# Every fourth weight slab's low part on GpSimd, in a transformer block pair of split-precision matmuls

## The chip, the cores and the metric

One core of a Trainium2 chip. The time is device microseconds of one execution of the whole program; several runs of the kernel are timed, and one more execution is taken with the hardware profiler. TensorE (PE) multiplies, VectorE (DVE), ScalarE (ACT) and GpSimd (POOL) do elementwise work, and DMA queues are issued from SyncE (SP), ScalarE and GpSimd. PEld in the profile is TensorE's loading of weights.

## The reference

Two transformer blocks on 256 tokens of width 2048, all in float32. What matters here is that nearly all of the work is products of a 256 x K activation with a large weight matrix:

```
# block 1
proj = rms_norm(x) @ w_in                     # 2048 x 7168
mixed = concat(diff_attention, hgrn2) @ w_out # 2048 x 2048
x = x + rms_norm(mixed)
x = x + rms_norm(cross_attention(x, mem))     # w_cq, w_ckv, w_co
x = x + rms_norm((silu(h @ w_gate) * (h @ w_up)) @ w_ffn_out)   # hidden 5632
# block 2
z = rms_norm(x) @ w_in_2                      # 2048 x 11280
y = gates_a * (pool_mixer @ w_branch_a) + gates_b * (gated_linear_attention @ w_branch_b)
x = x + rms_norm(y @ w_out_2)
x = x + rms_norm((silu(h @ w_ffn_gate) * (h @ w_ffn_up)) @ w_ffn_down)
```

Each weight element is used once for each of the 256 tokens, so all weights (some 0.5 GB) pass through SBUF once.

## The kernel before

**The matmuls.** A float32 product is made of three products of reduced type (float32r): with each operand split into a high part, which is the value rounded, and a low part, which is the rest, it is high x high + high x low + low x high. Activations are split when they are transposed (`split_T`, lines 307 to 324: ScalarE makes the high part, VectorE the low part). Weights are split as they arrive.

**Slabs.** A slab is 256 rows (two chunks of 128) by 512 columns of a weight matrix, 512 KB. `wsub` (lines 367 to 377) fetches one: SyncE issues the DMA into a `raw` buffer (line 371), ScalarE casts it into the high part `wh` (line 375), and VectorE subtracts to make the low part `wl` (line 376). There are four `raw` buffers and eight each of `wh` and `wl` (lines 33 and 34), taken in rotation. A raw buffer can be refilled when its cast and its subtraction are done; a `wh` or `wl` buffer when TensorE has used it.

**Groups.** `group` (lines 385 to 395) computes 512 columns of the output for both halves of the tokens (two tiles of 128): it asks for all slabs of the group, eight of them where K is 2048 (six or four elsewhere), and then multiplies. `mm_both` (lines 397 to 410) goes through the slabs once and does both token tiles for each chunk: 2 chunks x 3 products x 2 tiles = 12 matmuls a slab. With `apart` it is `mm` (lines 413 to 426): all slabs for tile 0, then all for tile 1, which is used at the boundaries between sublayers, where the second tile's input is not there yet.

**Order.** The kernel is written in one stream, and a scheduler puts each engine's instructions in the order of priorities, as far as their inputs are expected to be ready. `ahead` (lines 379 to 383) gives the slabs of a group a priority 50 instructions earlier than the place where they stand, so that they are prepared during the group before; at a boundary (`self.bound`) it gives them none. Each engine's queue, and each DMA queue, is in order when it runs. Beside the matmuls run small jobs that advance by a `tick` after every chunk: the decay attention (`decay_attn`, lines 506 to 596, called the lanes below), the softmax attention (lines 678 to 732), transposes, norms and the gating of the FFN (line 908). The lanes use VectorE at lines 535, 541, 543 and 550 and TensorE at line 516.

**Boundaries.** Between sublayers the outputs of a group are squared and summed, normalised with `rsqrt_mean` (lines 283 to 296) and added to x on VectorE (`add_normed`, lines 484 to 491, line 490), transposed on TensorE (line 304) and split (lines 322 and 323), before the next weight product can begin.

**GpSimd.** It sets a few buffers at the start, makes the identity, and issues DMAs: the setup vectors (line 195), the bias table (lines 263 and 273), the rows of mem (line 785), the broadcast gains (line 279) and the spilled x (line 948). It does no elementwise work on the weights.

Of the kernel before, what the change touches and what calls it, by code (L numbers as in the profile page):

```python
# [10 lines left out]
F32 = mybir.dt.float32  # L11
# [3 lines left out]
ALU = mybir.AluOpType  # L15
# [66 lines left out]
class Builder:  # L82
    def __init__(self, ctx, tc, A, out):
        self.tc, self.nc, self.A, self.out = tc, tc.nc, A, out
        e = ctx.enter_context
        self.cp = e(tc.tile_pool(name="const", bufs=1))
        self.ap = e(tc.tile_pool(name="acts", bufs=ACT_UNITS))
        self.rawp = e(tc.tile_pool(name="raw", bufs=RAW_BUFS))
        self.spp = e(tc.tile_pool(name="split", bufs=SPLIT_BUFS))
        self.smp = e(tc.tile_pool(name="small", bufs=16))  # L90
        self.psm = e(tc.tile_pool(name="psm", bufs=4, space=bass.MemoryType.PSUM))
        self.pss = e(tc.tile_pool(name="pss", bufs=4, space=bass.MemoryType.PSUM))
        self.n = 0
        self.junk = self.cp.tile([P, CW], F32, name="junk")
        self.jobs, self.lane, self.bound = [], [], False

# [270 lines left out]
    def wsub(self, W, k0, c0, ncol=CW):  # L367

        nc = self.nc
        raw = self.rawp.tile([P, 2, CW], F32, name=self.nm("raw"), tag="raw")  # L370
        nc.sync.dma_start(raw[:, :, :ncol],
                          W[k0 * P:(k0 + 2) * P, c0:c0 + ncol].rearrange("(k p) n -> p k n", p=P))
        hi = self.spp.tile([P, 2, CW], F32R, name=self.nm("wh"), tag="wh")
        lo = self.spp.tile([P, 2, CW], F32R, name=self.nm("wl"), tag="wl")
        nc.scalar.copy(hi[:, :, :ncol], raw[:, :, :ncol])  # L375
        nc.vector.tensor_tensor(lo[:, :, :ncol], raw[:, :, :ncol], hi[:, :, :ncol].bitcast(F32), ALU.subtract)  # L376
        return hi, lo

    def ahead(self):
# [782 lines left out]
```

## Time and profile before

| what | value |
|---|---|
| median of 3 runs | 2867.55 us (2867.44 to 2868.36) |
| the profiled execution, its own time | 2868.51 us |
| span of the profile, first to last instruction | 2866.7 us |
| TensorE matmul busy | 2836.1 us (99%) |
| VectorE busy | 1619.9 us (57%) |
| ScalarE busy | 1412.8 us (49%) |
| GpSimd busy | 44.7 us (2%) |
| read from HBM | 522.86 MB, 184 GB/s over the span |
| mean granted TensorE clock | 0.998 |

How to read it: busy time is the time in which an engine had an instruction under way. TensorE is covered to 99%, which by itself does not say that it runs at its peak, since the ends of matmuls are modelled; but where it is covered without a gap, another engine's saving cannot shorten the run. In the rows below, a timeline row gives the start, the duration, the engine and line, the operation, out<-in by the program's names and the number of instructions merged; in square brackets stands how long the engine had been idle before and what ended that.

### The profile page before, as it was taken

What the parts mean: (1) busy time and instruction counts of PE and PEld (TensorE: products, weight loads), DVE (VectorE), ACT (ScalarE), POOL (GpSimd) and SP (SyncE); (2) the same over time, 40 slices, a digit from 0 to 9 for tenths busy, and PEclk for the clock granted to TensorE, in tenths of its full rate; (3) what the DMA queues carried; (4) which work ended last, traced back from release to release, by engine and by line L of the source; (5) the groups of instructions that cost most, each with busy time, mean ns of one, the idle gap of its engine ahead of it and who ended that gap; (6) DMA issues with size and microseconds to landing.
All of it is one profiled execution on the core that took longest, in us unless ns stands there. A gap on an engine that the chain in (4) does not pass through costs nothing.

```text
span 2866.7 us, 35013 instructions
## 1 busy us (share of the span) xinstructions
PE 2836.1 (99%) x13196; PEld 2351.4 (82%) x13196; DVE 1619.9 (57%) x2147; ACT 1412.8 (49%) x2100; POOL 44.7 (2%) x89
## 2 busy tenths in 40 slices
PE   8999999999999999999999999999999999999998
PEld 6788888778888888888888898888888888888887
DVE  6666586665444455456665566555565444555455
ACT  6554575664444443445655475444464444443443
POOL 1000000000000000000000000000000000000000
PEclk9999999999999999999999999999999999999999
DMA  7555546546656666665655557666747666666663
GB/s 236 164 176 165 179 157 205 172 129 207 192 190 196 187 190 192 194 202 186 200 154 166 159 151 215 196 194 192 231 138 233 187 192 194 186 190 194 195 201 121
DMA packets 274922, 530.94 MB, mean 185 GB/s; under 512 B 17513, under 2 KB 29413, under 8 KB 274752
## 3 DMA queue, kind: packets, MB, share of 16 engines
q1 hardware_dynamic: 269040, 512.70, 58.6%
q0 software_dynamic: 5136, 14.95, 1.7%
q8 instruction: 103, 1.69, 0.2%
q10 hardware_dynamic: 576, 1.05, 0.1%
q14 instruction: 67, 0.55, 0.1%
HBM read 522.86 MB, written 5.77 MB: 184 GB/s over the span
## 4 chain that ended last, share of the span: by engine, by line
PE 94%; ACT 2%; DMA 1%; DVE 1%; issue 1%; SPq 0%; DVEq 0%; ACTq 0%
PE mm L407 83%; PE tp L304 2%; PE lps L516 2%; PE mm L422 2%; PE mm L423 2%; PE mm L424 2%; ACT junk L299 1%; ACT hi L322 1%; DVE wl L376 1%; DMA raw<-w_ffn_in 1%; ACT wh L375 0%; PE po L581 0%; PE sc L686 0%; DMA raw<-w_in 0%; DMA x<-x 0%
## 5 line engine op out<-in xcount | busy, mean ns | idle before, releaser
L376 DVE TENSOR_TENSOR wl<-raw,wh 128x1024 fp32r<-128x1024 f32 (+1 forms) x968 | 1176.0, 1216 | 1076.8 <-ACT wh L375 1074.6
L375 ACT CAST wh<-raw 128x1024 fp32r<-128x1024 f32 (+1 forms) x968 | 1012.1, 1047 | 1184.3 <-PE mm L407 1092.7
L407 PE MATMUL mm<-wh,hi 128*128 128x512 f32 (+1 forms) x3504 | 1091.5, 392 | 0.0
L407 PE MATMUL mm<-wl,hi 128*128 128x512 f32 (+1 forms) x3504 | 1080.0, 389 | 0.0
L407 PE MATMUL mm<-wh,lo 128*128 128x512 f32 (+1 forms) x3504 | 1077.6, 388 | 0.0
L407 PEld LDWEIGHTS mm<-wh,lo 128*128 128x128 f32 x3504 | 657.1, 188 | 133.8 <-issue 0.2
L407 PEld LDWEIGHTS mm<-wl,hi 128*128 128x128 f32 x3504 | 656.5, 188 | 132.0 <-issue 0.5
L407 PEld LDWEIGHTS mm<-wh,hi 128*128 128x128 f32 x3504 | 648.6, 188 | 129.9 <-issue 5.8
L422 PE MATMUL mm<-wh,hi 128*128 128x512 f32 (+1 forms) x304 | 121.6, 400 | 1.4 <-ACT hi L322 0.9
L423 PE MATMUL mm<-wl,hi 128*128 128x512 f32 (+1 forms) x304 | 120.1, 395 | 0.3 <-DVE wl L376 0.2
L424 PE MATMUL mm<-wh,lo 128*128 128x512 f32 (+1 forms) x304 | 119.8, 394 | 0.0
L322 ACT ACTIVATE hi<-tp,vec 128x128 fp32r<-128x128 f32 x224 | 71.7, 381 | 12.4 <-DVE lo L323 8.2
L323 DVE SCALAR_TENSOR_TENSOR lo<-tp,vec,hi 128x128 fp32r<-128x128 f32 x224 | 68.3, 345 | 15.9 <-ACT hi L322 15.1
L422 PEld LDWEIGHTS mm<-wh,hi 128*128 128x128 f32 x304 | 57.8, 190 | 16.5 <-ACT hi L322 6.5
L424 PEld LDWEIGHTS mm<-wh,lo 128*128 128x128 f32 x304 | 57.6, 189 | 13.0 <-DVE lo L323 2.2
L423 PEld LDWEIGHTS mm<-wl,hi 128*128 128x128 f32 x304 | 57.9, 191 | 11.4 <-DVE wl L376 1.6
L516 PEld LDWEIGHTS lps<-qd,kd 128*128 128x128 f32 x448 | 58.3, 191 | 4.2 <-issue 0.3
L516 PE MATMUL lps<-qd,kd 128*128 128x64 f32 x448 | 56.2, 268 | 0.0
L333 ACT ACTIVATE tok<-mm,r 128x512 f32<-128x512 f32 x44 | 30.1, 690 | 33.6 <-PE mm L407 33.6
L903 ACT ACTIVATE sg<-mm,r 128x512 f32<-128x512 f32 x44 | 30.4, 690 | 28.8 <-PE mm L407 28.8
L312 ACT CAST hi<-tp 128x512 fp32r<-128x512 f32 x54 | 29.6, 589 | 21.5 <-PE tp L304 21.4
L535 DVE TENSOR_TENSOR e<-b 128x512 f32<-128x512 f32 x56 | 38.3, 683 | 0.0
(241 smaller groups left out, 1181.7 us busy)
## 6 DMA issues: line engine op xcount, KB each, us to landing
raw<-w_in SPq DMA_DIRECT2D x256, 512.0 KB, 3.7
raw<-w_ffn_in SPq DMA_DIRECT2D x176, 512.0 KB, 3.8
raw<-w_ffn_out SPq DMA_DIRECT2D x88, 512.0 KB, 3.7
raw<-w_ffn_gate SPq DMA_DIRECT2D x88, 512.0 KB, 3.7
raw<-w_ffn_up SPq DMA_DIRECT2D x88, 512.0 KB, 3.7
raw<-w_ffn_down SPq DMA_DIRECT2D x88, 512.0 KB, 3.8
raw<-w_out SPq DMA_DIRECT2D x64, 512.0 KB, 4.2
raw<-w_branch_b SPq DMA_DIRECT2D x32, 512.0 KB, 3.8
```

What stands on the lines that cost most here:

```text
L304: self.nc.tensor.transpose(ps[:, i, :], src[:, i * P:(i + 1) * P], self.ident)
L322: nc.scalar.activation(hi[:, i, :], ps[:, i, :], AF.Copy, scale=g)
L323: nc.vector.scalar_tensor_tensor(lo[:, i, :], ps[:, i, :], g, hi[:, i, :].bitcast(F32), ALU.mult, ALU.subtract)
L375: nc.scalar.copy(hi[:, :, :ncol], raw[:, :, :ncol])
L376: nc.vector.tensor_tensor(lo[:, :, :ncol], raw[:, :, :ncol], hi[:, :, :ncol].bitcast(F32), ALU.subtract)
L407: nc.tensor.matmul(ps[t][:, :ncol], hT[t][kk // 4][p][:, kk % 4, :], w[:, i, :ncol], start=kk == first and p == 0 and w is wh, stop=kk == ...
L422: nc.tensor.matmul(ps[:, :ncol], xh, wh[:, i, :ncol], start=kk == first, stop=False)
L423: nc.tensor.matmul(ps[:, :ncol], xh, wl[:, i, :ncol], start=False, stop=False)
L424: nc.tensor.matmul(ps[:, :ncol], xl, wh[:, i, :ncol], start=False, stop=kk == last)
L516: nc.tensor.matmul(ps[:, h, :], lhs[:, i, :], rhs[:, i, :], start=c == 0, stop=c == cph - 1)
L535: nc.vector.tensor_tensor(ev, bv, bv[:, :, hh - 1:hh].to_broadcast([P, 4 * nb, 2 * hh]), ALU.subtract)
L903: nc.scalar.activation(u, ps, AF.Silu, scale=rstd[t])
```

## The change

Low parts of weight slabs are counted in the order in which the program asks for them; every fourth is computed on GpSimd instead of VectorE, by the same instruction on the same operands. Nothing else is touched.

```diff
-        self.n = 0
+        self.n = self.nsub = 0
...
         nc.scalar.copy(hi[:, :, :ncol], raw[:, :, :ncol])
-        nc.vector.tensor_tensor(lo[:, :, :ncol], raw[:, :, :ncol], hi[:, :, :ncol].bitcast(F32), ALU.subtract)
+        self.nsub += 1
+        eng = nc.gpsimd if self.nsub % 4 == 0 else nc.vector
+        eng.tensor_tensor(lo[:, :, :ncol], raw[:, :, :ncol], hi[:, :, :ncol].bitcast(F32), ALU.subtract)
         return hi, lo
```

## Rows read from the trace of the kernel before

**Rows 1.** The head of the page: busy us, share of the span, instructions of an engine.
```profile
span 2866.7 us, 35013 instructions
PE 2836.1 (99%) x13196; PEld 2351.4 (82%) x13196; DVE 1619.9 (57%) x2147; ACT 1412.8 (49%) x2100; POOL 44.7 (2%) x89
```

**Rows 2.** The waits of PE: us in total, times, longest us.
```profile
PE tp L304 <- DVE hh L908: 1.8, 1, 1.8
...
PE tp L304 <- DVE mg L490: 0.9, 1, 0.9
...
PE mm L423 <- DVE wl L376: 0.2, 1, 0.2
```

**Rows 3.** The waits of all engines, the longest of them.
```profile
ACT wh L375 <- PE mm L407: 1092.7, 705, 2.8
```

**Rows 4.** The chain that ended last, in the first FFN: start us, us.
```profile
753.01 43.54 PE mm L407 x192
```

**Rows 5.** The page's costliest groups: busy, mean ns | idle before, releaser.
```profile
L376 DVE TENSOR_TENSOR wl<-raw,wh 128x1024 fp32r<-128x1024 f32 (+1 forms) x968 | 1176.0, 1216 | 1076.8 <-ACT wh L375 1074.6
```

**Rows 6.** The groups of POOL: its one instruction that reads SBUF.
```profile
masks.py:199 POOL TENSOR_SCALAR_AFFINE_SELECT ident<-ident 128x128 f32<-128x128 f32 x1 | 0.3, 283 | 0.0
```

**Rows 7.** The page's DMA issues: xcount, KB each, median us to landing.
```profile
raw<-w_ffn_gate SPq DMA_DIRECT2D x88, 512.0 KB, 3.7
```

**Rows 8.** The timeline of the start: ACT, PE and POOL.
```profile
16.52 1.05 ACT L375 CAST wh<-raw 128x1024 fp32r<-128x1024 f32 x1
...
25.15 1.11 PE L304 MATMUL tp<-ident,x 128*128 128x128 f32 x4 [3.09 <-DMA x<-x]
...
28.48 1.04 ACT L375 CAST wh<-raw 128x1024 fp32r<-128x1024 f32 x1 [0.25 <-DMA raw<-w_in]
...
25.03 0.51 POOL L195 DMA_DIRECT2D vec_rows<-cross_pre_g  x1 [20.12 <-DVE vec_rows L192]
...
32.65 0.54 POOL L233 DMA_DIRECT2D onehot<-c_onehot  x1
...
34.13 0.39 PE L423 MATMUL mm<-wl,hi 128*128 128x512 f32 x1
```

**Rows 9.** The timeline of the boundary into the first FFN: ACT, DVE and PE.
```profile
616.36 1.15 ACT L375 CAST wh<-raw 128x1024 fp32r<-128x1024 f32 x1
...
619.43 1.22 DVE L376 TENSOR_TENSOR wl<-raw,wh 128x1024 fp32r<-128x1024 f32 x1
...
620.82 0.15 DVE L487 TENSOR_REDUCE pssq<-acc 128x1 f32<-128x4 f32 x1
...
619.50 0.50 PE L423 MATMUL mm<-wl,hi 128*128 128x512 f32 x1 [0.22 <-DVE wl L376]
...
621.01 0.39 PE L423 MATMUL mm<-wl,hi 128*128 128x512 f32 x1
...
623.25 0.99 PE L304 MATMUL tp<-ident,mg 128*128 128x128 f32 x5 [0.91 <-DVE mg L490]
```

**Rows 10.** The timeline of DVE at the end of a group in the first FFN.
```profile
790.87 1.22 DVE L376 TENSOR_TENSOR wl<-raw,wh 128x1024 fp32r<-128x1024 f32 x1 [1.49 <-ACT wh L375]
793.59 1.23 DVE L376 TENSOR_TENSOR wl<-raw,wh 128x1024 fp32r<-128x1024 f32 x1 [1.50 <-ACT wh L375]
```

**Rows 11.** The groups of DVE: the lanes' instructions with two SBUF inputs.
```profile
L535 DVE TENSOR_TENSOR e<-b 128x512 f32<-128x512 f32 x56 | 38.3, 683 | 0.0
...
L543 DVE TENSOR_TENSOR qd<-fT,e 128x256 f32<-128x256 f32 x56 | 23.5, 419 | 0.0
```

**Rows 12.** The timeline of a lane's step: its product on DVE, and PE's load.
```profile
150.63 0.42 DVE L543 TENSOR_TENSOR qd<-fT,e 128x256 f32<-128x256 f32 x1
...
151.44 0.54 PEld L516 LDWEIGHTS lps<-qd,kd 128*128 128x128 f32 x3
```

## The prediction

> **What bounds the kernel now.** I read the head of the page first, then TensorE's own waits, then the stretches in which it waits. TensorE (PE) is busy for 2836.1 of 2866.7 us, VectorE (DVE) for 57% of the span, GpSimd (POOL) for 44.7 us [rows 1]. So the work that the change moves is on an engine that has room, and goes to one that is nearly empty; neither is the bound. The waits of TensorE say how much a faster VectorE could return at most: 1.8 us on a product of line 908, 0.9 us on the normalised rows of line 490, and 0.2 us, once in the whole run, on a low part [rows 2]. That is 2.9 us for the rows that name VectorE with a price worth having.
>
> Why the low parts are never late: ScalarE, which makes the high part, waited 705 times for TensorE's matmuls, 1092.7 us in all [rows 3]. It waits for one of the eight split buffers. A slab is 12 matmuls, and 192 matmuls (16 slabs) take 43.54 us [rows 4], so a slab is consumed in 2.72 us. A buffer that comes free is filled at once and read seven slabs later, 19.0 us. Less the cast (1.05 us) and the subtraction (1.22 us, the mean of all 968 is 1216 ns [rows 5]) some 16.8 us are left. Only where a group gets no head start (the start, and the four boundaries between sublayers) can a low part be needed as soon as it is made.
>
> **What the change does, and the price of one.** 968 low parts [rows 5], every fourth: 242 instructions leave VectorE, 242 x 1.216 = 294 us, and 242 come to GpSimd. No operand, buffer or DMA is added. The counter runs in program order and most groups have eight slabs, so it is the fourth and eighth of a group, and always the same of the four raw buffers. What one costs on GpSimd the trace does not show. GpSimd's only instruction that reads SBUF took 283 ns for 128 elements of one input [rows 6], so 1024 elements would be 8 x 283 = 2.3 us as a plain multiple, and 4.5 us if a second input doubles it. From below, nothing in the rows makes it faster than VectorE's 1.2 us. I take 2.3 us, the plain multiple, and keep 1.2 and 4.5 as ends. The Trainium skill (GPSIMD Engine Reference, Performance versus the Vector engine) gives 4497 ns for 2048 elements of this kind; half of that is an estimate of 2.25 us, and no run here shows it.
>
> **Steady groups: 0.** 2.3 instead of 1.2 us comes out of 16.8 us of cover; even 4.5 us does. GpSimd is then busy 242 x 2.3 = 557 us, a fifth of the span. If the cover were gone, each of the 242 would cost its 1.1 us, 266 us. The queue of loads (SP) must now wait for GpSimd before it refills every fourth raw buffer, and it is in order, so three later loads stand behind that one. A turn of the ring is 4 x 2.72 = 10.9 us, and needs 3.7 us of landing [rows 7], 1.05 us of cast and 2.3 us: 7.1 us, with 3.8 us to spare.
>
> **GpSimd's own queue: 0.** Its DMA issues can now stand behind a low part that waits for its high part. The broadcast rows are asked for a group (21.8 us) ahead of use. The eight loads of mem (line 785) are used two ticks later and are the exposed ones: 0 to 8 x 2.3 = 18 us if each is met. TensorE has no wait on them now, so I take 0.
>
> **Start: +0.7.** The fourth slab's high part ends at 16.52 + 1.05 = 17.57 us, GpSimd has nothing to do until 25.03, so its low part ends near 19.9 us (22.1 at the upper end); TensorE next stands still until 25.15 us for the second half of x [rows 8]. Hidden. The eighth: its high part ends at 28.48 + 1.04 = 29.52, but GpSimd is issuing setup DMAs until 32.65 + 0.54 = 33.19, and TensorE reads that low part at 34.13. In front of those issues it ends at 31.8 and costs 0; behind them at 35.5, +1.4 us (at 4.5 us a piece 37.7, +3.6). I take the middle of the two orders, +0.7, and keep 0 to +3.6.
>
> **Boundary into the first FFN: -0.9.** The last slab there (the 184th) has its high part at 616.36 + 1.15 = 617.51, but VectorE reaches it only at 619.43 and ends at 620.65, with TensorE reading at 621.01 [rows 9]. GpSimd would start at 617.5 and end at 619.8: earlier, though each one is slower. VectorE loses the 1.22 us that stand in front of the sum of line 487, from which the 0.91 us wait for line 490 follows; I take all 0.9 back. The bad end: the 183rd slab is what TensorE already waited 0.22 us for; if GpSimd's instruction holds VectorE up until 619.8, that subtraction ends at 621.1 where TensorE had it at 619.50, +1.6 us.
>
> **Attention lanes: +1.** There VectorE's queue is dense and its products go to TensorE soon. The move takes 1.2 us of every four slabs off VectorE, a gain that rows 2 have nothing to pay for. Bounds 0 to +27, from the second rival; I take +1, near zero, since the waits of TensorE contain no lane matmul.
>
> **Sum.** 0.7 - 0.9 + 1 = +0.8 us. The profiled execution took 2868.51 us (its span is 2866.7), so 2869.3 by its clock; it stands 0.96 above the median of 2867.55, so on the medians' scale the forecast is 2868.4 us.
>
> **Rivals.** (1) *VectorE's relief pays at the boundaries.* Every wait in rows 2 goes: 2867.55 - 2.9 = 2864.6. It needs no low part late anywhere. To be faster by more than 0.2% it would need 5.7 us, twice what these rows hold, so it would have to come from a better order of TensorE's instructions. Against it: the other 2836.1 us are TensorE's busy time, which the change does not touch.
>
> (2) *A wait takes the place of the work removed: GpSimd's low part blocks VectorE in the lanes.* Mechanism: both read SBUF, and while GpSimd holds the read, a VectorE instruction with two SBUF inputs stands still. In the FFN there is room: low parts stand 2.72 us apart (790.87, 793.59 [rows 10]), and what VectorE does in between at a group's end (lines 908 and 313) has one operand in PSUM. In the lanes lines 535 and 543 run 112 times with two SBUF inputs [rows 11]. GpSimd is busy 2.3 of every 10.9 us, 21%; 112 x 0.21 = 24 are met, for half of 2.3 us on average: 27 us of delay on VectorE. It decides where TensorE wants the product within that 1.15 us: one product ends at 151.05 and the weight load of line 516 starts at 151.44, 0.39 us later [rows 12], and then the rest is a stall. All of them: 2895. Half of them, the case I price: +13.5, 2881.9. A third: +9, 2877. For it: such thin margins. Against: VectorE's queue is also 1.2 us shorter per four slabs, which the same lane gets back. The Trainium skill (SBUF — State Buffer, Who interferes with whom) says that a VectorE instruction with two SBUF inputs contends with a GpSimd instruction that reads SBUF and that the later of the two blocks fully. By that rule this is the likelier way; no row of the kernel before can show it, since its GpSimd runs nothing of the kind beside VectorE.
>
> (3) *GpSimd becomes the bound.* From 10.9 - 3.7 - 1.05 = 6.1 us per low part the ring of raw buffers stalls TensorE; at 7 us it would be 242 x 0.9 = +218 us. It needs nearly three times my price.
>
> **Chances.** No change that can be measured (0.2%, 5.7 us, is about what a measurement of this kernel can tell): 0.74. Slower: 0.20, nearly all of it (2), with 0.02 for (3). Faster: 0.06. The likeliest case alone spans 2864.6 (rival 1) to 2867.55 + 3.6 + 1.6 + 1 = 2873.8. The range reaches up to 2878, past a third of the lanes' delay; above it lie (3) and half of (2), about 0.1, and below it the few cases of a better order.
>
> **What would show it.** Right: line 376 on GpSimd 242 times at 2 to 3 us; VectorE down by some 290 us; TensorE's busy time unchanged; the wait of ScalarE for TensorE still the longest. Rival 2: VectorE's lines 376, 535, 541 and 543 with longer means than now, and new waits of TensorE on lane products. Rival 3: TensorE waiting for wl on GpSimd in the FFN. I am wrong if TensorE's waits on VectorE and GpSimd together grow by more than 6 us, or if the span falls below 2861.

## The result: slower by 1.45%, and the profile after

| what | before | after |
|---|---|---|
| median of 3 runs | 2867.55 us | 2908.51 us (2908.04 to 2908.98) |
| ratio, 95% interval | | 1.0145, 1.0130 to 1.0159 |
| the profiled execution, its own time | 2868.51 us | 2908.04 us |
| span of the profile | 2866.7 us | 2906.2 us |
| mean granted TensorE clock | 0.998 | 0.995 |

The forecast was 2868.4 us with a range to 2878.0; the time came out 41 us above the kernel before and 30.5 us above the range. From line 378 on, line numbers after are two higher than before.

The head of the page after, to be read against [rows 1]:

```profile
span 2906.2 us, 35034 instructions
...
PE 2842.2 (98%) x13196; PEld 2356.3 (81%) x13196; DVE 1413.7 (49%) x1905; ACT 1413.1 (49%) x2100; POOL 624.7 (21%) x331
```

The work moved as the diff says, and GpSimd is far from full. But the span grew by 39.5 us, TensorE's busy time by only 6.1, and VectorE's fell by 206 us although 294 us of work had left it. The low parts themselves, in the page's costliest groups (busy, mean ns, then the idle time ahead of them):

```profile
L378 DVE TENSOR_TENSOR wl<-raw,wh 128x1024 fp32r<-128x1024 f32 (+1 forms) x726 | 888.2, 1225 | 1177.6 <-ACT wh L375 1176.1
...
L378 POOL TENSOR_TENSOR wl<-raw,wh 128x1024 fp32r<-128x1024 f32 (+1 forms) x242 | 581.3, 2402 | 2216.4 <-ACT wh L375 2216.4
```

One low part takes 2.40 us on GpSimd. VectorE's remaining 726 kept almost their mean of [rows 5], which accounts for some 6 us of the missing 88. The other 82 are in other instructions of VectorE. First its groups before, of the kinds that got longer:

```profile
L541 DVE TENSOR_TENSOR kd<-fT,e 128x256 f32<-128x256 f32 x28 | 11.8, 421 | 2.0 <-ACT e L536 2.0
...
L490 DVE SCALAR_TENSOR_TENSOR mg<-mg,r,x 128x512 f32<-128x512 f32 x16 | 10.9, 747 | 0.1
...
L361 DVE TENSOR_SCALAR sd<-sd 128x512 f32<-128x512 f32 x16 | 6.8, 423 | 1.7 <-ACT sd L360 1.7
...
L1072 DVE TENSOR_TENSOR gate<-gate,gate 128x512 f32<-128x512 f32 x8 | 5.1, 686 | 0.0
```

And the same view after, with the lanes' instructions that [rows 11] showed (lines 535 and 543 there are 537 and 545 here, and line 541 is 543):

```profile
L537 DVE TENSOR_TENSOR e<-b 128x512 f32<-128x512 f32 x56 | 40.5, 722 | 0.0
...
L910 DVE SCALAR_TENSOR_TENSOR hh<-mm,r,sg 128x512 f32<-128x512 f32 x44 | 31.0, 746 | 3.8 <-PE mm L409 3.8
L543 DVE TENSOR_TENSOR kd<-fT,e 128x256 f32<-128x256 f32 x28 | 23.2, 830 | 18.2 <-ACT e L538 18.2
L545 DVE TENSOR_TENSOR qd<-fT,e 128x256 f32<-128x256 f32 x56 | 23.2, 415 | 0.0
...
L492 DVE SCALAR_TENSOR_TENSOR mg<-mg,r,x 128x512 f32<-128x512 f32 x16 | 15.2, 1008 | 0.1
L361 DVE TENSOR_SCALAR sd<-sd 128x512 f32<-128x512 f32 x16 | 14.8, 924 | 14.0 <-ACT sd L360 14.0
L1074 DVE TENSOR_TENSOR gate<-gate,gate 128x512 f32<-128x512 f32 x8 | 13.8, 1760 | 0.0
```

The same instructions on the same shapes take up to 2.6 times as long (1760 for 686 ns in the sum of the gates). Line 910, with one operand in PSUM, took 746 ns after and 747 before. A stretched duration here is not work but time in which the instruction stood still, and it counts as busy. So VectorE's 49% overstates what it does.

The waits of TensorE after (us in total, times, longest), against [rows 2]:

```profile
PE tp L304 <- DVE mg L492: 8.9, 6, 1.9
PE tp L304 <- DVE gate L1074: 8.3, 4, 2.1
PE tp L304 <- DVE sg L969: 5.9, 4, 1.7
...
PE tp L304 <- DMA mem<-mem: 4.0, 1, 4.0
...
PE tp L304 <- DVE yg L492: 1.9, 1, 1.9
...
PE lps L518 <- DVE qd L545: 1.3, 2, 0.9
...
PE tp L304 <- DVE sg L655: 1.1, 1, 1.1
PE xps L518 <- DVE qx L566: 1.1, 1, 1.1
...
PE mm L425 <- POOL wl L378: 0.3, 1, 0.3
```

Added up over all rows of this view, TensorE's waits for VectorE grew from 7.3 to 37.7 us, those for DMAs from 8.2 to 11.0, all others from 3.6 to 4.8: +34.4. (The 7.3 us hold 3.6 for the setup vectors and 0.8 of small waits, which the 2.9 us of the prediction leave out.) With 6.1 us more of busy time that is 40.5, one us above the growth of the span. A low part that is late costs 0.3 us in the whole run. What is late is work of VectorE that ends in a transpose: the rows on mg, gate, sg and yg make 26.1 us, the lanes' qd and qx 2.4.

The row names the last instruction before the transpose, which is not always the one that was held. In the timeline after, the last one was itself held at the four gates (8.3 us) and at three of the sums on mg (1.9 us each): 14.0 us. At the other three waits for mg and the one for yg, 5.1 us, one of the 128x1 products of `rsqrt_mean` was held (lines 291, 292 and 295, 1.4 to 1.9 us for 0.16) and the sum behind it ran at its usual speed. At all five waits for sg, 7.0 us, it was the tensor_scalar of line 361, which has one SBUF input and stands three steps ahead (two of ScalarE, one of VectorE). The first wait for line 969 in the timeline after:

```profile
1675.02 1.98 POOL L378 TENSOR_TENSOR wl<-raw,wh 128x832 fp32r<-128x832 f32 x1 [11.88 <-ACT wh L375]
1675.51 1.78 DVE L361 TENSOR_SCALAR sd<-sd 128x512 f32<-128x512 f32 x1 [1.66 <-ACT sd L360]
...
1679.86 0.68 DVE L969 TENSOR_TENSOR sg<-sg,hn 128x512 f32<-128x512 f32 x1
...
1680.69 0.63 PE L304 MATMUL tp<-ident,sg 128*128 128x128 f32 x4 [1.45 <-DVE sg L969]
```

Line 361 took 1.78 us there for 0.42 before, and ended at 1677.29, 0.29 us after GpSimd's low part; line 969 kept its 0.68 us and was only late.

A place where the last instruction itself was held, the sum of the gates in branch b, in the timeline after:

```profile
1925.68 1.29 DVE L1073 TENSOR_TENSOR gate<-mm,gate 128x512 f32<-128x512 f32 x2
...
1926.88 3.44 DVE L1074 TENSOR_TENSOR gate<-gate,gate 128x512 f32<-128x512 f32 x2
...
1927.08 2.69 POOL L378 TENSOR_TENSOR wl<-raw,wh 128x1024 fp32r<-128x1024 f32 x1 [8.50 <-ACT wh L375]
...
1930.38 1.01 PE L304 MATMUL tp<-ident,gate 128*128 128x128 f32 x4 [2.03 <-DVE gate L1074]
```

and the same place before:

```profile
1902.87 1.29 DVE L1072 TENSOR_TENSOR gate<-gate,gate 128x512 f32<-128x512 f32 x2
...
1903.62 1.26 PE L304 MATMUL tp<-ident,gate 128*128 128x128 f32 x8
```

The two sums took 1.29 us together and now take 3.44. GpSimd's low part runs from 1927.08 to 1929.77; the second sum ends at 1930.32, 0.55 us after it, a little less than the 0.69 us of a free sum. It stood still until GpSimd was done, and TensorE with it for 2.03 us. What comes behind the wait is in the stretches of the windows (us, then busy time of PE, PEld, DVE, ACT, POOL, then the granted clock, DMA share, GB/s):

```profile
1928.00:1931.00 3.00, 0.97 (x8) 0.73 (x7) 2.92 (x2) 0.59 (x1) 1.77 (x1) 0.92 0.31 117
1931.00:1934.00 3.00, 3.00 (x9) 2.43 (x8) 0.91 (x2) 1.63 (x2) 0.00 (x0) 0.51 0.55 171
1934.00:1937.00 3.00, 3.00 (x14) 2.48 (x14) 1.01 (x1) 0.92 (x1) 0.00 (x0) 1.00 0.25 66
```

After the standstill the granted clock is 0.51, the lower level (1.2 GHz), for some 3 us, in which 9 matmuls are done instead of 14. Behind three of the four gates it is so, behind the one at 1978.64 it stays 1.00. Over the three the clock gave away 4.8 us, worked out from the windows as below for e7. It also fell behind the wait for mem (0.72 and 0.71 from 362.5 to 368.5 us, 1.7 us given away) and behind the one on yg (0.51 from 1361 to 1364 us, 1.5 us). At the start, from 24 to 33 us, it gave away 3.4 us before and 1.7 after. Together that is some 6 us more, about TensorE's 6.1 us more of busy time.

### The profile page after: what moved, and what is told of

It reads as the page before. It is cut to its first block, busy times and chain, and to the rows that moved or that the text cites. A ratio compares the mean times of both kernels' runs of the same rounds, so it can differ in the third digit from the quotient of the medians.

```text
span 2906.2 us, 35034 instructions
## 1 busy us (share of the span) xinstructions
PE 2842.2 (98%) x13196; PEld 2356.3 (81%) x13196; DVE 1413.7 (49%) x1905; ACT 1413.1 (49%) x2100; POOL 624.7 (21%) x331
## 4 chain that ended last, share of the span: by engine, by line
PE 88%; DVE 5%; ACT 4%; issue 2%; DMA 1%; POOL 0%; SPq 0%; DVEq 0%; ACTq 0%; POOLq 0%
PE mm L409 80%; PE tp L304 2%; PE lps L518 2%; ACT wh L375 1%; PE mm L424 1%; PE mm L426 1%; PE mm L425 1%; ACT hi L322 1%; DVE wl L378 1%; ACT junk L299 1%; DMA raw<-w_in 1%; DVE mg L492 1%; DVE gate L1074 0%; DVE sd L361 0%; PE po L583 0%
## 5 line engine op out<-in xcount | busy, mean ns | idle before, releaser
L378 DVE TENSOR_TENSOR wl<-raw,wh 128x1024 fp32r<-128x1024 f32 (+1 forms) x726 | 888.2, 1225 | 1177.6 <-ACT wh L375 1176.1
L378 POOL TENSOR_TENSOR wl<-raw,wh 128x1024 fp32r<-128x1024 f32 (+1 forms) x242 | 581.3, 2402 | 2216.4 <-ACT wh L375 2216.4
L313 DVE TENSOR_TENSOR lo<-tp,hi 128x512 fp32r<-128x512 f32 x54 | 35.2, 686 | 31.5 <-ACT hi L312 31.5
```

What stands on the lines that cost most here:

```text
L313: nc.vector.tensor_tensor(lo, ps, hi.bitcast(F32), ALU.subtract)
L378: eng.tensor_tensor(lo[:, :, :ncol], raw[:, :, :ncol], hi[:, :, :ncol].bitcast(F32), ALU.subtract)
```

## The experiments

The theory (theory 1 in what was expected of the runs): while GpSimd's low part reads SBUF, VectorE's instructions with two SBUF inputs stand still, and it costs where TensorE wants one of them at once. Rivals: the lower rate of GpSimd or the other order of the instructions is what costs; or the queue of GpSimd's DMA issues is (theory 2 there).

**e1: GpSimd is as busy, but does not read.** Every fourth low part is computed for 2 of 512 columns only and GpSimd writes zeros twice over the rest, so most of each of these low parts is left out.

```diff
+        if self.nsub % 4 == 0:
+            nc.gpsimd.tensor_tensor(lo[:, :, :2], raw[:, :, :2], hi[:, :, :2].bitcast(F32), ALU.subtract)
+            for _ in range(2):
+                nc.gpsimd.memset(lo[:, :, 2:ncol].bitcast(F32), 0.0)
...
```

> Every fourth low part is left to GpSimd as in the changed kernel, but GpSimd subtracts only the first two columns of each row chunk and fills the rest with zeros, twice over, so that it is busy about as long (some 2.1 us in place of 2.4 us) while it reads next to nothing. Its place in the queue and its wait on the cast stay. This leaves most of every fourth low part out. Theory 1, GpSimd's reading of SBUF holds up VectorE's instructions with two SBUF inputs: most of the 41 us goes, the kernel takes 2868 to 2882 us (what is left is the mem loads that stand behind low parts in GpSimd's queue, some 6 us, and what hangs on the order), and VectorE's line of the gate sum falls from a mean of 1760 ns to about 690 ns. Theory 2, the loss comes from GpSimd's queue, from the scheduler's new order of the instructions or from the low part being late: nothing of that changes, 2900 to 2910 us.

Measured: 2870.23 us beside 2867.03, ratio 1.0010 (1.0001 to 1.0020). Its groups of GpSimd, and the gates' sum on VectorE:

```profile
L380 POOL MEMSET wl<- 128x1020 f32 (+1 forms) x484 | 457.1, 945 | 2179.4 <-PE mm L413 2030.2 <-PE mm L429 136.0
L378 POOL TENSOR_TENSOR wl<-raw,wh 128x4 fp32r<-128x4 f32 x242 | 54.3, 224 | 67.7 <-ACT wh L375 67.5
```

```profile
L1078 DVE TENSOR_TENSOR gate<-gate,gate 128x512 f32<-128x512 f32 x8 | 5.1, 683 | 0.0
```

GpSimd is occupied for 2 x 0.945 + 0.224 = 2.1 us per low part, nearly as long as in the changed kernel, and 38 of the 41 us are gone. The gates' sum is back at 683 ns. One thing is not as it was expected: the zeros do not wait for the cast, so they run first, as soon as TensorE frees the buffer, and GpSimd is busy at another time than in the changed kernel. That this is not the reason shows at the gates: the zeros are written from 1904.50 to 1906.46 us, the first of two sums begins within them, at 1905.91, and the two take 1.28 us together. So it is the reading that costs, not that GpSimd is busy or that VectorE has less to do. The memsets still hold up something: the tensor_scalar of line 646 took 626 ns in the mean for 422 before.

**e2: the same reads in four pieces.** GpSimd computes the low part in quarters, two per row chunk.

```diff
+            h = ncol // 2
+            for i in range(2):
+                for a, b in ((0, h), (h, ncol)):
+                    nc.gpsimd.tensor_tensor(lo[:, i, a:b], raw[:, i, a:b], hi[:, i, a:b].bitcast(F32), ALU.subtract)
...
```

> GpSimd's low part in four instructions of 256 elements in place of one of 1024. Theory 1 with a hold that lasts for one GpSimd instruction: a VectorE instruction that meets one waits for at most a quarter, about 0.7 us, and the kernel comes to 2875 to 2890 us, with the gate sum's mean below 1200 ns. If the next GpSimd instruction takes the read again before VectorE gets it, or if the two share it instead of locking it: no better than 2900 us. Theory 2 (queue, order, lateness): 2905 us or a little more, since four instructions take longer than one.

Measured: 2886.01 us beside 2867.03, ratio 1.0067 (1.0052 to 1.0082). Its groups of GpSimd and of the gates' sum, then its wait for the gates:

```profile
L381 POOL TENSOR_TENSOR wl<-raw,wh 128x256 fp32r<-128x256 f32 (+1 forms) x968 | 729.8, 784 | 2050.9 <-ACT wh L375 2039.1 <-ACT y L288 11.7
```

```profile
L1079 DVE TENSOR_TENSOR gate<-gate,gate 128x512 f32<-128x512 f32 x8 | 7.3, 952 | 0.0
```

```profile
PE tp L304 <- DVE gate L1079: 1.8, 4, 0.5
```

GpSimd reads longer in all (4 x 0.784 = 3.1 us for 2.4), and yet the loss is less than half. The hold lasts for one GpSimd instruction: a sum waits for at most the piece under way (952 ns for 1760), and the longest wait at a gate falls from 2.1 to 0.5 us. VectorE's busy time is 1411.9 us, for 1413.7 in the changed kernel: it is held about as long in all, and what falls is the single hold. GpSimd's low parts, longer now, came late twice (2.0 us of TensorE's waits). Behind a gate's short wait the clock stays up (1.00 from 1917 to 1924 us); it fell once in this run, behind a wait of 2.66 us at a transpose of mem.

**e3 and e4: where in the run it costs.** A flag is set in the groups of the FFNs, except the first of each.

```diff
-        eng = nc.gpsimd if self.nsub % 4 == 0 else nc.vector
+        eng = nc.gpsimd if self.nsub % 4 == 0 and self.inffn else nc.vector       # e3
+        eng = nc.gpsimd if self.nsub % 4 == 0 and not self.inffn else nc.vector   # e4
```

> GpSimd gets its every fourth low part only within the two FFNs, without their first group: 128 of the 242. Theory 1: nothing that runs on VectorE beside them there has two SBUF inputs, apart from line 933 in the last block (the gain), and TensorE has 17 us of cover, so 2866 to 2871 us, the same as before the change. Rival, each moved low part costs the same 41/242 = 0.17 us wherever it stands: +22 us, 2889 us.

> The complement of the run with the FFNs alone: every fourth low part on GpSimd everywhere except there, 114 of the 242. Theory 1, the cost stands where GpSimd's reading meets VectorE's two-input instructions: the whole loss is here, 2903 to 2911 us. Rival, the cost goes with the number: 114/242 of 41 us, 2886 us.

Measured: e3, with 128 low parts on GpSimd, 2866.65 us beside 2867.03, ratio 0.9997 (0.9988 to 1.0006). e4, with the other 114, 2908.42 us beside 2865.86, ratio 1.0146 (1.0131 to 1.0161): all of the loss. In e3 GpSimd's low part stands beside VectorE like this (its timeline at the end of a group):

```profile
793.93 2.39 POOL L379 TENSOR_TENSOR wl<-raw,wh 128x1024 fp32r<-128x1024 f32 x1 [8.49 <-ACT wh L376]
795.18 1.29 DVE L314 TENSOR_TENSOR lo<-tp,hi 128x512 fp32r<-128x512 f32 x2 [1.23 <-ACT hi L313]
```

The splits of line 314 have one operand in PSUM and run through, 1.29 us for two, beside GpSimd's 2.39. Only one group was held: yg of line 936, with two SBUF inputs (the gain in the last block), takes 962 ns for 685, and TensorE does not wait for it. There is no gain either: VectorE's relief has no taker.

**e5: another phase.** The second and sixth slab of a group of eight go to GpSimd instead of the fourth and eighth; as many instructions, as much reading.

```diff
-        eng = nc.gpsimd if self.nsub % 4 == 0 else nc.vector
+        eng = nc.gpsimd if self.nsub % 4 == 2 else nc.vector
```

> The same number of low parts, but the second and sixth slab of each group of eight instead of the fourth and eighth, so that GpSimd is not at work when a group ends. Theory 1: the four gate sums of the second branch, some 3.6 us each with TensorE's clock, come free, as do the multiplications by the gate of line 969, and the kernel takes 2880 to 2895 us; the gate sum's mean falls to about 690 ns. Something else may collide in their place in the lanes. Theory 2, the loss goes with the number of low parts on GpSimd and not with when they run: 2905 to 2912 us.

Measured: 2893.66 us beside 2867.03, ratio 1.0095 (1.0078 to 1.0111). The gates' sum is free again and TensorE no longer waits for it; other places are still met, line 969 among them (3.0 us for 5.9; here line 966 ahead of it is held, 1186 ns for 691), which was expected to come free. The group, and the two longest waits of this kind:

```profile
L1074 DVE TENSOR_TENSOR gate<-gate,gate 128x512 f32<-128x512 f32 x8 | 5.2, 685 | 0.0
```

```profile
PE tp L304 <- DVE mg L492: 7.2, 5, 2.1
...
PE tp L304 <- DVE sg L969: 3.0, 4, 1.6
```

Which slab is moved decides which sum is met. In the change as made, the eighth slab of a group always falls where the gates end their group, so all four gates were met.

**e6: mem's loads leave GpSimd's queue.** In the changed kernel they stand behind low parts that wait for their high part. The timeline of GpSimd, and of TensorE's transposes of mem, after:

```profile
355.06 2.39 POOL L378 TENSOR_TENSOR wl<-raw,wh 128x1024 fp32r<-128x1024 f32 x1 [11.37 <-ACT wh L375]
357.40 1.62 POOL L787 DMA_DIRECT2D mem<-mem  x3
...
362.58 0.63 PE L304 MATMUL tp<-ident,mem 128*128 128x128 f32 x4 [3.99 <-DMA mem<-mem]
```

Three loads leave together once the low part is done, and TensorE waits 3.99 us for mem. At 384.88 us, at another transpose of mem, it waits 2.50 us for the split (line 323).

```diff
-                    nc.gpsimd.dma_start(u, A["mem"][0, t * P:(t + 1) * P, j * CW:(j + 1) * CW])
+                    nc.sync.dma_start(u, A["mem"][0, t * P:(t + 1) * P, j * CW:(j + 1) * CW])
```

> The changed kernel, with the eight loads of mem issued by SyncE instead of GpSimd, so that they no longer stand behind low parts. Theory 2 for its share: TensorE's waits of 4.0 us for a mem load and 2.5 us behind one go, and 4 to 9 us with them, 2900 to 2905 us. Rival, those waits only take the place of others that come later in the same stretch (the boundary after it gives time back): 2906 to 2910 us, no difference that counts.

Measured: 2901.77 us beside 2865.86, ratio 1.0123 (1.0108 to 1.0138). Against 1.0145 that is some 6 us, but the two intervals overlap. In the trace the waits for mem fall by 1.5 us only (4.0 to 2.5: on SyncE its loads are issued between weight loads), and the wait at the other transpose from 2.5 to 0.8. So a queue term is likely, of some 3 us by these waits and at most some 6 by the medians; the rest of the difference is not settled.

**e7: the gates alone.** Only in branch b, where the gates are, do low parts go to GpSimd: 16 in the whole run.

```diff
-        eng = nc.gpsimd if self.nsub % 4 == 0 else nc.vector
+        eng = nc.gpsimd if self.nsub % 4 == 0 and self.second else nc.vector
...
+            self.second = br == 1
...
```

> Low parts go to GpSimd only in the eight groups of the second branch of block 2 (16 of the 242). Theory 1: each of the four gate sums is held up, TensorE waits some 2.1 us for each and runs at the lower clock behind it, 3.6 us a time as between the groups of the two traces, so +13 to +15 us, 2880 to 2882 us. If only the wait counts: 4 x 2.1 = +8.4 us, 2875.5 us. Rival, the cost goes with the number: 16 x 0.17 = +2.7 us, 2870 us.

Measured: 2877.98 us beside 2865.86, ratio 1.0038 (1.0024 to 1.0052), +12.1 us. The wait, in its waits of TensorE:

```profile
PE tp L305 <- DVE gate L1075: 8.6, 4, 2.4
```

and the windows behind the second and third gate:

```profile
1949.00:1952.00 3.00, 2.83 (x11) 2.31 (x12) 1.41 (x3) 1.63 (x2) 0.00 (x0) 0.66 0.48 175
1952.00:1955.00 3.00, 3.00 (x12) 2.40 (x11) 1.23 (x1) 0.10 (x1) 0.00 (x0) 0.77 0.21 60
1997.50:2000.50 3.00, 2.95 (x10) 2.49 (x11) 1.20 (x2) 1.28 (x2) 0.00 (x0) 0.54 0.53 175
2000.50:2003.50 3.00, 3.00 (x13) 2.46 (x12) 1.23 (x1) 0.58 (x2) 0.00 (x0) 0.89 0.04 5
```

The waits cost 8.6 us. What the clock gave away in these four windows is 3 x (0.34 + 0.23 + 0.46 + 0.11) = 3.4 us; behind the other two gates it stayed 1.00. Together 12.0 us, beside 12.1 by the medians; that it fits to a tenth is luck, since the clock at the start, which differs from trace to trace, gave away 1.7 us here for 3.4 before, and the span grew by 9.2 us only. The loss is a little under the 13 to 15 us that were expected, where each gate had the lower clock behind it. Sixteen low parts out of 242 make three tenths of the loss.

**e8: e1 and e6 together,** to see whether e1's last 3 us are the queue. The diff is those of e1 and e6, with the same parts left out as in e1.

> The kernel in which GpSimd reads next to nothing (most of every fourth low part is left out), with the loads of mem issued by SyncE as well. If the 3 us that stayed without the reading are the mem loads behind GpSimd's work: 2865 to 2868 us, as before the change. Rival, they are the order of the instructions or the start: 2869 to 2872 us.

Measured: 2867.84 us beside 2865.86, ratio 1.0006 (0.9996 to 1.0015). The interval takes in 1, so no loss is shown, but it overlaps that of e1, so whether e1's 3 us are mem's queue, the start or another order of instructions stays open.

## Why the prediction was wrong

**Price of one: right.** 2.3 us was taken, 2.40 measured (the 16 of e7 2.45).

**Steady groups: right.** 0 was said; e3 gives 0.9997 for 128 of the 242, and low parts that come late cost TensorE 0.3 us in all. The third rival, GpSimd as the bound, fell: it is busy for 21%.

**Start: +0.7, near enough.** The eighth low part, whose lateness the step priced, ran between the setup DMAs, from 30.17 to 32.58 us, and TensorE waited 0.26 us for it. TensorE's other waits there are for x and the setup vectors; that for x fell from 5.3 to 4.2 us, that for vec rose from 3.6 to 4.2, -0.5 together. Both move about from kernel to kernel (5.9 and 2.2 in e6). New small waits for lines 323 and 333 (0.7 and 1.4 us up to 54 us) were not in the step.

**GpSimd's own queue: 0, wrong by a little.** The reason "TensorE has no wait on them now" said nothing of a queue in which a load stands behind an instruction that itself waits 11 us for its input. It is one wait of 4.0 us, likely another of 2.5, and 1.7 us that the clock gave away behind the first; the bounds of 0 to +18 held it.

**Boundary into the first FFN: -0.9, wrong in sign.** VectorE's relief was not to be had, since the hold takes it back at the same place. The whole stretch lies some 15 us later after the change. The 184th low part, whose removal was to give the 0.9 us back, runs on GpSimd from 634.80 us and holds a 128x1 product of the norm, behind which the sum of the second token tile comes late:

```profile
634.80 2.38 POOL L378 TENSOR_TENSOR wl<-raw,wh 128x1024 fp32r<-128x1024 f32 x1 [10.94 <-ACT wh L375]
...
635.37 1.84 DVE L291 TENSOR_TENSOR t<-y 128x1 f32<-128x1 f32 x1
...
640.12 0.66 PE L304 MATMUL tp<-ident,mg 128*128 128x128 f32 x4 [1.83 <-DVE mg L492]
```

TensorE waits 1.83 us here where [rows 9] had 0.91. At the first tile of the same boundary the low part before it (620.23 to 622.89) holds one of the four normalised sums, and TensorE waits 1.91 us where it had not waited at all. The bad end of that step named the hold, but for a low part on VectorE; it met the norm and the sums.

**"Attention lanes: +1 (...) Bounds 0 to +27, from the second rival": this is the step that failed.** The mechanism of that rival is what happened, and I had even said that by the rule of the page it is the likelier way; I gave it 0.2 and placed it wrongly. I looked for instructions with two SBUF inputs in the lanes alone, because VectorE's queue is dense there. The lanes' products were indeed held (line 541, 543 after, from 421 to 830 ns). Their delay on VectorE, 22 us over lines 535, 541 and 543, is not far from the 27 us of the rival; but TensorE's waits for the lanes are 2.4 us and not half of it, so nearly always it had other matmuls to do. What counts is not where VectorE is dense but where TensorE takes its result next with nothing else to do, and these are the chains of elementwise steps that end in a transpose: the sums of the gates, the norms and sums of the normalised rows, and the sigmoids ahead of the gated products sg, 26.1 us. I listed none of them, though the waits of [rows 2] name lines 490 and 908 at the end of just such a chain. Nor would a list of two-input instructions have found all: 7.0 us of it come from line 361 with one. The price was mis-sized too: half a GpSimd instruction on average was assumed for one that is met by chance; the phase of the counter made it nearly a full one at every gate (e5 against the change).

**A term that was missing.** Behind a wait of some 2 us the granted clock fell to its lower level for a while. The sum had nothing for it; in the changed kernel it adds 4.8 us at the gates and some 3 us behind mem and yg, and in e7 3.4 us to the 8.6 of the waits.

**The skill's rule.** The Trainium skill (SBUF — State Buffer, Who interferes with whom) says that a VectorE instruction with two SBUF inputs contends with a GpSimd instruction that reads SBUF and not with one that only writes, that the shared pair of ports is an exclusive lock, and, where it speaks of VectorE's two-port modes, that whichever issues first has the pair for its whole instruction. Change, e1 and e2 agree, for two inputs: 1760, 683 and 952 ns for the same sum. The weight given to it should have been near one for the mechanism; only its price had to come from the profile.

## What to carry to other kernels

Before work that reads SBUF goes to GpSimd, list every VectorE instruction with two SBUF operands, and the tensor_scalars from SBUF to SBUF too, and ask which of them lie on a chain whose end TensorE waits for at once, first of all the chains that end in a transpose at the end of a group; the total load of either engine says nothing about this. Where the move is wanted, choose the stretches in which VectorE's instructions have an operand in PSUM (e3 costs nothing), choose the phase, and cut the GpSimd instruction into pieces (e2). And an engine that issues DMAs in order should not be given elementwise work that waits for its input without asking which loads stand behind it.

## What was not expected of the hardware

- The hold is not for two inputs alone: the tensor_scalar of line 361, one SBUF input to SBUF, went from 423 to 924 ns. GpSimd's writes alone hold such an instruction (422 to 626 ns on line 646 of e1), but not a two-input one (683). The same section of the Trainium skill counts tensor_scalar among those that can take the shared pair; these rows agree.
- Tiny ones are held as well: the 128x1 products of line 291 went from 156 to 345 ns in the mean, and one of them that met a low part took 1.84 us.
- It goes both ways: the low part in the gates' timeline took 2.69 us instead of 2.39, and the first of the two sums was under way when it began. All fifteen low parts that took over 2.5 us began while an instruction of VectorE with two SBUF inputs was under way.
- A wait of about 2 us was followed by the lower clock behind three of four gates in the changed kernel and two of four in e7, and not behind the 1.91 us at the boundary (1.00 from 621 to 630 us). The length of the wait does not decide it: the same wait of 1.91 us on mg was followed by it in e4 (at 537.45 us; 0.85 and 0.59 from 537 to 543) and not in the changed kernel (at 536.07). What does, no run here shows.
